# The Newton steps of the channel mixers' norm columns on VectorE in place of GpSimd

## The chip, the cores and the metric

The kernel runs on one core of a Trainium2 chip. The metric is the device time of one execution in microseconds, as the median of three runs. A core has a matrix engine (TensorE; PE in the profile, PEld its weight loads), VectorE (DVE), ScalarE (ACT), GpSimd (POOL) and SyncE (SP), which here issues the loads. Each engine works through its own instructions in order and waits for others by semaphores.

## The reference, cut to what matters

A decoder trunk of two layers on 512 tokens of width 1024, in float32. Each layer is a channel mixer, a token mixer and another channel mixer, so there are four channel mixers, numbered 0 to 3 (`idx` in the code):

```python
def rmsnorm(x, g):
    x32 = x.astype(jnp.float32)
    y = x32 * lax.rsqrt(jnp.mean(x32 * x32, axis=-1, keepdims=True) + RMS_EPS)
    return y.astype(x.dtype) * g

def swiglu(x, w_gate, w_up, w_down):
    return (jax.nn.silu(x @ w_gate) * (x @ w_up)) @ w_down

h = h + 0.5 * swiglu(rmsnorm(h, ffn_norm_a[i]), ...)   # before the token mixer
h = h + 0.5 * swiglu(rmsnorm(h, ffn_norm_b[i]), ...)   # after it
```

The hidden width of the channel mixers is 2816. The token mixers (latent attention in layer 0, sparse attention in layer 1) are not touched.

## The kernel before, in words

**Layout.** The residual stream `h` is held transposed: 8 tiles of 128 features by 512 tokens. A float32 product is made from three products of a high and a low part (`hi` is a rounded copy by ScalarE, `lo` the remainder, by a subtraction on VectorE). The weights are split in the same way: `wslab` (L132) loads a tile `wr`, ScalarE copies it (L143), VectorE makes the remainder (L145).

**The norm.** The products are made from the unnormed `h` (times the gains), and the factor 1/sqrt(mean square) of each token is applied afterwards. For a channel mixer the factor must be there as a `row`: 128 equal partitions by 512 tokens. It is made in these steps:

- squares and their sum over the features. In mixers 1 to 3 ScalarE squares, GpSimd adds into `s2` (L254), and `norm_col` (L273) sums over partitions on TensorE into 128x4 values `pc` (L278). In mixer 0, ScalarE squares the input in token order and sums along the row (L422), which gives the 128x4 values directly;
- `rsqrt` (L256): three instructions on VectorE (L259 to L261) make a first guess from the bits of the float, and three Newton steps refine it. Each round is four instructions on GpSimd (L264 to L267) where `pool` is set, three on VectorE (L269 to L271) where it isn't. All are on 128x4 values, in the tile `small`;
- `norm_bcast` (L286): eight TensorE instructions (four matmuls in the program, L290) spread the column over a PSUM bank `pb`, and ScalarE copies it to `row` (L450).

**Where this stands in a channel mixer** (`ffn`, L368). The first three of 22 hidden tiles are made by plain products (`plain`, L356: L364 to L366), gate and up for each, into `pg` and `pu`. In mixers 1 to 3 the column is asked for behind the two plain products of the first tile. In mixer 0 it is asked for behind those of the second. The broadcast stands on TensorE behind the second tile's products, and the third tile's follow it. The gate of each tile (L377 to L379) needs `row`. Meanwhile VectorE makes the operands of the remaining 19 tiles: `combine` (L236 to L238 and a split, L170 and L171) sums pieces of the activations, and `wsums` (L308, with L338 to L342) pieces of the weights, for a scheme of seven products in place of eight (L352 to L354). After that come the down projections (L162 to L164, added to `h` in L401).

**What sets the order.** The kernel is written through a framework that orders each engine's instructions by a planner: of the instructions that are ready, by its own model of time, the one that was written first goes first. So the order of VectorE's instructions is not the written one; where a short chain waits for its own last step, an instruction that is ready is put between. Buffers of a tag are used in turn: a weight tile's copy waits until TensorE has used the tile that it replaces.

Of the kernel before, what the change touches and what calls it, by code (L numbers as in the profile page):

```python
# [20 lines left out]
D = 1024  # L21
# [40 lines left out]
class Kern:  # L62
# [305 lines left out]
    def ffn(self, idx, gain_next, ap, tp):  # L368
# [5 lines left out]
        def gate(f, g):  # L374

            t = tg[f] = tp.tile([P, S], F32, tag="tg", bufs=2, name="tg")
            nc.vector.tensor_tensor(t, g, row, op=ALU.mult)  # L377
            nc.scalar.activation(t, t, AF.Silu, scale=-1.0)
            nc.vector.tensor_tensor(t, t, row, op=ALU.mult)  # L379
# [4 lines left out]
        def act(f):  # L384
            t = tu[f]
            if f < PLAIN:
                t = tu_tile()
                nc.vector.scalar_tensor_tensor(t, tu[f], -1.0, tg[f], op0=ALU.mult, op1=ALU.mult)
            else:
                nc.vector.tensor_tensor(t, t, tg[f], op=ALU.mult)  # L390
            ah[f] = ap.tile([P, S], F32R, tag="act", bufs=4 * NG, name="ah")
            al[f] = ap.tile([P, S], F32R, tag="act", bufs=4 * NG, name="al")
            self.split(t, ah[f], al[f])
# [19 lines left out]
        sums, xts = self.small_sums, []  # L413

        def tokens(t):

            xts.append(tp.tile([P, D], F32, tag="fr", bufs=3, name="xt"))
            with self.tc.issue_after(self.high.ins):
                nc.scalar.dma_start(xts[t], a["x_tok"][t * P : (t + 1) * P, :])

        def squares(t):
            nc.scalar.activation(xts[t], xts[t], AF.Square, accum_out=sums[:, t : t + 1])  # L422
# [7 lines left out]
        for f, g in enumerate(gates):  # L430
            u = tu[f] = self.bank(("mm", "S")[f % 2], "pu")
            self.plain(idx, f, 0, g)
            if f == 1 and idx == 0:

                squares(0)
                tokens(3)
                squares(1)
            self.plain(idx, f, 1, u)
            if f == 0:
                for c in self.late:  # L440
                    self.sumsq(self.h[c])
                col = self.norm_col(D, self.s2, pool=True) if idx else None
            elif f == 1:
                if idx == 0:
                    squares(2)
                    squares(3)
                    col = self.rsqrt_col(sums, D, pool=True)
                pb = self.norm_bcast(col)
                row = tp.tile([P, S], F32, tag="row", bufs=1, name="row")
                nc.scalar.activation(row, pb, AF.Copy)  # L450
                for e in range(2):
                    gate(e, gates[e])
                    act(e)
            else:
                gate(f, g)
                act(f)
            for p in (((0,), (1,), (2, 3)) if idx else ((0, 1), (2,), (3,)))[f]:
                self.combine(p)
# [842 lines left out]
```

## Time and profile before

| | us |
|---|---|
| median of three runs | 1926.41 |
| the runs | 1928.86, 1926.41, 1923.17 |
| span of the profiled execution | 1920.1 |
| TensorE busy | 1876.1 |
| VectorE busy | 1518.9 |
| ScalarE busy | 1091.4 |
| GpSimd busy | 334.9 |

The span runs from the first to the last instruction of one execution; the page has no device time of that execution beside it, and the three runs are 3.1 to 8.8 us above it. In a row of a timeline stand the start and the duration in us, the engine, the line of the kernel, the operation, the tile written and the tiles read, the shapes, and how often. A bracket is the time for which the engine was idle before, and what it waited for. A row of a list of waits has who waited for whom, the total in us, how often, and the longest.

### The profile page before, as it was taken

The page shows a single profiled execution, that of the slowest core. Times are in us where ns is not written, and L with a number is a line of the kernel's source. Part 1 is how long each engine was busy: PE and PEld are TensorE (multiplying, and loading weights), DVE is VectorE, ACT ScalarE, POOL GpSimd, SP SyncE. Part 2 cuts the span into 40 slices and gives each one's busy share as a digit, 9 for nine tenths or more (in the row PEclk, how much of TensorE's full clock was granted, in tenths as well). Part 3 has the DMA queues.
Part 4 walks back from the last instruction along what each step waited for, and adds up shares of the span by engine and source line. Part 5 has one row for each costly group of instructions (what it writes and reads, how often), then busy time and mean ns, then how long its engine had stood idle before and what let it go on. Part 6 is the DMA issues. An engine that isn't in the chain of part 4 may idle for free. (4 is left out here: it accounts for less than half of the span.)

```text
span 1920.1 us, 33220 instructions
## 1 busy us (share of the span) xinstructions
PE 1876.1 (98%) x12584; PEld 1707.3 (89%) x12584; DVE 1518.9 (79%) x2838; ACT 1091.4 (57%) x2040; POOL 334.9 (17%) x421
## 2 busy tenths in 40 slices
PE   8999999999999999999999999999999999999998
PEld 8999999878888999998999999877788888999997
DVE  7988886678778888876888888655987978888885
ACT  7555554478665555555555555435877865555553
POOL 1000000257631000002200000114666531000000
PEclk9999999999999999999999999999999999999999
DMA  6433321311233333323333332243122133333321
GB/s 224 140 100 99 113 90 42 110 50 42 73 116 111 100 100 109 112 62 107 117 110 108 104 100 79 65 123 100 51 67 67 40 118 96 108 112 108 104 76 67
DMA packets 75904, 183.28 MB, mean 95 GB/s; under 512 B 9040, under 2 KB 37072, under 8 KB 75744
## 3 DMA queue, kind: packets, MB, share of 16 engines
q1 hardware_dynamic: 72800, 176.39, 29.6%
q10 hardware_dynamic: 2944, 4.77, 0.7%
q8 instruction: 99, 1.62, 0.3%
q14 instruction: 61, 0.50, 0.1%
HBM read 178.96 MB, written 2.16 MB: 94 GB/s over the span
## 5 line engine op out<-in xcount | busy, mean ns | idle before, releaser
L254 POOL TENSOR_TENSOR s<-s,sq 128x512 f32<-128x512 f32 x38 | 55.7, 1466 | 988.2 <-ACT sq L250 985.2
L163 PE MATMUL pd<-al,wd 128*128 128x512 f32 x576 | 225.0, 391 | 0.0
L162 PE MATMUL pd<-ah,wd 128*128 128x512 f32 x576 | 224.8, 390 | 0.0
L164 PE MATMUL pd<-ah,wd 128*128 128x512 f32 x576 | 224.6, 390 | 0.0
L171 DVE TENSOR_TENSOR w<-wr,w 128x1024 fp32r<-128x1024 f32 x72 | 88.1, 1224 | 134.1 <-ACT w L170 134.1
L352 PE MATMUL px<-four,wh 128*128 128x256 f32 x608 | 168.5, 277 | 0.0
L354 PE MATMUL pq<-four,wl 128*128 128x256 f32 x608 | 167.9, 276 | 0.3 <-DVE wl L171 0.3
L354 PE MATMUL px<-four,wl 128*128 128x256 f32 x608 | 168.0, 276 | 0.0
L353 PE MATMUL px<-four,wh 128*128 128x256 f32 x608 | 167.9, 276 | 0.0
L352 PE MATMUL pq<-four,wh 128*128 128x256 f32 x608 | 167.9, 276 | 0.0
L353 PE MATMUL pq<-four,wh 128*128 128x256 f32 x608 | 167.8, 276 | 0.0
L143 ACT ACTIVATE w<-wr 128x1024 fp32r<-128x1024 f32 (+5 forms) x120 | 100.6, 844 | 104.7 <-issue 20.1
L401 DVE SCALAR_TENSOR_TENSOR h<-pd,h 128x512 f32<-128x512 f32 x216 | 148.0, 685 | 13.8 <-PE pd L164 13.7
L170 ACT ACTIVATE wd<-wdr 128x384 fp32r<-128x384 f32 x192 | 99.3, 519 | 101.4 <-ACT wd L170 62.9
L164 PEld LDWEIGHTS pd<-ah,wd 128*128 128x128 f32 x576 | 108.2, 188 | 22.9
L162 PEld LDWEIGHTS pd<-ah,wd 128*128 128x128 f32 x576 | 108.1, 188 | 20.3
L163 PEld LDWEIGHTS pd<-al,wd 128*128 128x128 f32 x576 | 108.1, 188 | 19.7
L145 DVE TENSOR_TENSOR w<-wr,w 128x1024 fp32r<-128x1024 f32 (+4 forms) x81 | 83.3, 1031 | 48.8 <-ACT w L143 48.2
L171 DVE TENSOR_TENSOR wd<-wdr,wd 128x384 fp32r<-128x384 f32 x192 | 105.7, 552 | 18.6 <-ACT wd L170 18.3
L639 ACT ACTIVATE p<-p,small 128x512 f32<-128x512 f32 (+1 forms) x192 | 106.8, 558 | 21.0 <-DVE small L638 17.3
L352 PEld LDWEIGHTS px<-four,wh 128*128 128x128 f32 x608 | 114.1, 188 | 0.9 <-ACT pg L477 0.5
L354 PEld LDWEIGHTS pq<-four,wl 128*128 128x128 f32 x608 | 114.1, 188 | 0.7 <-DVE wl L171 0.7
(359 smaller groups left out, 6281.1 us busy)
## 6 DMA issues: line engine op xcount, KB each, us to landing
wr<-in_w_gu SPq DMA_DIRECT2D x96, 512.0 KB, 3.3
ru<-in_w_gu SPq DMA_DIRECT2D x76, 512.0 KB, 4.2
wdr<-in_w_down SPq DMA_DIRECT2D x192, 192.0 KB, 2.4
wr<-in_w_down SPq DMA_DIRECT2D x24, 256.0 KB, 2.6
wr<-in_mla_w_o SPq DMA_DIRECT2D x8, 512.0 KB, 3.3
wr<-in_nsa_w_q SPq DMA_DIRECT2D x8, 512.0 KB, 3.3
th<-btab_d SPq DMA_DIRECT2D x16, 256.0 KB, 3.6
wr<-in_nsa_w_o SPq DMA_DIRECT2D x8, 512.0 KB, 3.6
```

The lines of the kernel that those rows point to most:

```text
L143: self.copied = nc.scalar.activation(wh[:, m], raw[:, m], AF.Copy)
L145: nc.vector.tensor_tensor(wl[:, m], raw[:, m], f32v(wh[:, m]), op=ALU.subtract)
L162: mm(out, wh, xh, start=first, stop=False)
L163: mm(out, wh, xl, start=False, stop=False)
L164: return mm(out, wl, xh, start=False, stop=last)
L170: nc.scalar.activation(hi, src, AF.Copy)
L171: (nc.gpsimd if pool else nc.vector).tensor_tensor(lo, src, f32v(hi), op=ALU.subtract)
L352: mm(out, wh[:, p], xh, start=first and p == 0, stop=False, skip_group_check=True)
L353: mm(out, wh[:, p], xl, start=False, stop=False, skip_group_check=True)
L354: mm(out, wl[:, p], xh, start=False, stop=last and p == KP - 1, skip_group_check=True)
L401: nc.vector.scalar_tensor_tensor(self.h[c], p, 0.5, self.h[c], op0=ALU.mult, op1=ALU.add)
L639: nc.scalar.activation(p_sb[:, :n], p_sb[:, :n], AF.Exp, bias=nm, scale=-1.0, accum_out=sm)
```

## The change

Both calls in `ffn` that set `pool=True` lose it: that of mixers 1 to 3 through `norm_col`, and that of mixer 0 directly. The twelve GpSimd instructions on 128x4 values per mixer (a square, a product, a scale and shift, a product, three times) become nine on VectorE, of the form that the token mixers' norms use already. No other call sets `pool` for the norm, so the GpSimd branch is not used any more.

```diff
             if f == 0:
                 for c in self.late:
                     self.sumsq(self.h[c])
-                col = self.norm_col(D, self.s2, pool=True) if idx else None
+                col = self.norm_col(D, self.s2) if idx else None
             elif f == 1:
                 if idx == 0:
                     squares(2)
                     squares(3)
-                    col = self.rsqrt_col(sums, D, pool=True)
+                    col = self.rsqrt_col(sums, D)
                 pb = self.norm_bcast(col)
```

The two forms of a round:

```python
            if pool:
                nc.gpsimd.tensor_tensor(t, y, y, op=ALU.mult)
                nc.gpsimd.tensor_tensor(t, t, v, op=ALU.mult)
                nc.gpsimd.tensor_scalar(t, t, -0.5, 1.5, op0=ALU.mult, op1=ALU.add)
                nc.gpsimd.tensor_tensor(y, y, t, op=ALU.mult)
                continue
            nc.vector.scalar_tensor_tensor(t, y, -0.5, v, op0=ALU.mult, op1=ALU.mult)
            nc.vector.tensor_tensor(t, t, y, op=ALU.mult)
            nc.vector.scalar_tensor_tensor(y, t, 1.5, y, op0=ALU.add, op1=ALU.mult)
```

## The prediction

> **What bounds the kernel now.** I read the page's busy shares first, to see which engine has no room.
>
> ```profile
> span 1920.1 us, 33220 instructions
> PE 1876.1 (98%) x12584; PEld 1707.3 (89%) x12584; DVE 1518.9 (79%) x2838; ACT 1091.4 (57%) x2040; POOL 334.9 (17%) x421
> ```
>
> TensorE is busy for 1876.1 of 1920.1 us, so only 44 us of gaps can be won by moving work. VectorE has 401 us of idle time over the whole span, but that is an average. The next view is the list of waits of TensorE, and of its weight loads (PEld): total us, how often, the longest.
>
> ```profile
> PE pb L290 <- POOL small L267: 10.6, 4, 4.2
> PE pg L364 <- ACT w L143: 5.8, 1, 5.8
> ...
> PEld pb L290 <- POOL small L267: 11.4, 4, 4.4
> ```
>
> The largest wait of TensorE is on exactly the instructions that the change touches: four times it stands before the broadcast of the norm column (L290) until the last Newton step on GpSimd (L267) is done, 10.6 us in all (11.4 counted at the weight loads). The timeline of TensorE gives the four places. Each bracket is the idle time in front.
>
> ```profile
> 31.64 1.16 PE L290 MATMUL pb<-ident,small 128*128 128x128 f32 x8 [1.11 <-POOL small L267]
> 591.04 1.16 PE L290 MATMUL pb<-ident,small 128*128 128x128 f32 x8 [2.51 <-POOL small L267]
> 932.72 1.16 PE L290 MATMUL pb<-ident,small 128*128 128x128 f32 x8 [2.79 <-POOL small L267]
> 1591.08 2.07 PE L290 MATMUL pb<-ident,small 128*128 128x128 f32 x8 [4.18 <-POOL small L267]
> ```
>
> So TensorE was free at 30.53, 588.53, 929.93 and 1586.90 us. I call these places 1 to 4, one for each channel mixer. Why the column is late shows in the timeline of GpSimd, here the first and the last of the twelve steps at places 1 and 4:
>
> ```profile
> 25.11 0.20 POOL L264 TENSOR_TENSOR small<-small 128x4 f32<-128x4 f32 x1 [24.67 <-DVE small L261]
> ...
> 31.39 0.20 POOL L267 TENSOR_TENSOR small<-small 128x4 f32<-128x4 f32 x1
> ...
> 1580.30 6.39 POOL L264 TENSOR_TENSOR small<-small 128x4 f32<-128x4 f32 x1 [9.82 <-DVE small L261]
> ...
> 1590.83 0.20 POOL L267 TENSOR_TENSOR small<-small 128x4 f32<-128x4 f32 x1
> ```
>
> A step on 4 columns takes 0.20 us when it is free, but at place 4 the first one took 6.39. It ended at 1586.69. The timeline of VectorE for the same time shows what ended it:
>
> ```profile
> 1578.45 0.15 DVE L259 TENSOR_SCALAR small<-pc 128x4 f32<-128x4 f32 x1
> 1578.52 0.41 DVE L237 TENSOR_TENSOR u<-y,u 128x256 f32<-128x256 f32 x1
> 1578.85 0.16 DVE L260 TENSOR_SCALAR small<-small 128x4 int32<-128x4 int32 x1
> 1578.92 1.22 DVE L171 TENSOR_TENSOR wl<-ru,wh 128x1024 fp32r<-128x1024 f32 x1
> 1580.06 0.16 DVE L261 TENSOR_SCALAR small<-small 128x4 int32<-128x4 int32 x1
> 1580.13 1.22 DVE L145 TENSOR_TENSOR w<-wr,w 128x1024 fp32r<-128x1024 f32 x1
> 1581.26 1.22 DVE L171 TENSOR_TENSOR four<-u,four 128x1024 fp32r<-128x1024 f32 x1
> 1582.40 0.42 DVE L238 TENSOR_TENSOR u<-y,u 128x256 f32<-128x256 f32 x1
> 1582.73 0.68 DVE L171 TENSOR_TENSOR wl<-s,wh 128x512 fp32r<-128x512 f32 x1
> 1583.34 1.02 DVE L171 TENSOR_TENSOR wd<-wdr,wd 128x384 fp32r<-128x384 f32 x2
> 1584.28 1.22 DVE L171 TENSOR_TENSOR four<-u,four 128x1024 fp32r<-128x1024 f32 x1
> 1585.41 1.21 DVE L145 TENSOR_TENSOR w<-wr,w 128x1024 fp32r<-128x1024 f32 x1
> 1587.96 0.56 DVE L171 TENSOR_TENSOR wd<-wdr,wd 128x384 fp32r<-128x384 f32 x1 [1.34 <-ACT wd L170]
> ```
>
> From 1580.13 to 1586.62 VectorE runs two-input subtractions without a gap, and the first GpSimd step ends within 0.1 us of the first pause. GpSimd's steps are held up while VectorE is dense. [...]
>
> **The change part by part.** Removed: 4 x 12 steps on GpSimd, and with them TensorE's wait on L267. Added: 4 x 9 steps on VectorE (L269 to L271, three a round). No DMA moves, and nothing is moved past SP's queue. The price of the added steps is in the trace, since the token mixers already run this chain on VectorE:
>
> ```profile
> 359.37 0.16 DVE L269 SCALAR_TENSOR_TENSOR small<-small 128x4 f32<-128x4 f32 x1
> ...
> 359.84 1.23 DVE L145 TENSOR_TENSOR w<-wr,w 128x1024 fp32r<-128x1024 f32 x1
> 360.99 0.16 DVE L269 SCALAR_TENSOR_TENSOR small<-small 128x4 f32<-128x4 f32 x1
> ...
> 361.97 0.16 DVE L271 SCALAR_TENSOR_TENSOR small<-small 128x4 f32<-128x4 f32 x1
> ```
>
> The last six steps start between 360.99 and 361.97: 0.98 / 5 = 0.196 us from step to step. Nine in a row are 1.77 us. Where another instruction that is ready stands between two steps, a step holds VectorE for less: L259 to L237 above is 0.07 us, L260 to L171 0.07. So nine steps cost VectorE between 9 x 0.07 = 0.63 us (interleaved) and 1.77 us (in a row), per place.
>
> *Is the column in time?* In a row, the steps at place 4 would end at about 1580.06 + 0.20 + 1.77 = 1582.0, 4.9 us before TensorE is free. At worst the planner puts one ready instruction between any two steps, as it does with L259, L260 and L261 here. Eight ready instructions lie behind L261 (two in the row marked x2), which end at 1586.62. With eight steps between them at 0.07 that is 1587.2, and with a ninth behind them 1587.4: 0.5 us after 1586.90. I carry this worst case to all four places: a wait of 0 to 2.0 us stays of the 10.6. I take 0.3, near the low end, since at the other places fewer instructions stand before VectorE's pause, or TensorE comes later. Gain here: 10.3 us, between 8.6 and 11.4.
>
> *What stands behind the steps on VectorE?* The remainders of the weights (L145), which TensorE needs. At place 2 TensorE already waits for one:
>
> ```profile
> 581.65 0.16 DVE L261 TENSOR_SCALAR small<-small 128x4 int32<-128x4 int32 x1
> 581.72 1.21 DVE L145 TENSOR_TENSOR w<-wr,w 128x1024 fp32r<-128x1024 f32 x1
> ...
> 582.99 0.39 PE L366 MATMUL pu<-x,w 128*128 128x256 f32 x1 [0.78 <-DVE w L145]
> ```
>
> If all nine steps went ahead of this L145, TensorE would lose 1.77 us more there. At place 4 the same L145 ends at 1581.35, about when the product that uses it begins (1586.90 minus the 5.5 us from 582.99 to 588.53, a whole product less its first instructions). So two places are exposed, 3.5 us together. But L145 stands directly behind L261, that is, it was ready then, and takes the slot in which the first step waits for L261. I take 0.5 us of loss, between 0 and 3.5. The other instructions of the list are put off by 0.6 us or so, and the next product's L145 (1585.41) still ends before TensorE needs it behind the broadcast.
>
> [...]
>
> *The clock.* The granted clock is the third column from the right (here of TensorE alone; busy us, instructions, clock, DMA share, GB/s):
>
> ```profile
> 934.00:937.40 3.40, 3.40 (x18) 0.51 0.29 111
> 938.00:941.40 3.40, 3.40 (x33) 1.00 0.00 0
> 1592.90:1596.10 3.20, 3.20 (x17) 0.50 0.03 8
> 1597.00:1600.20 3.20, 3.20 (x31) 1.00 0.00 0
> ```
>
> Right after the gaps of 2.79 and 4.18 us TensorE ran at half clock for 3.4 us and more. It did 18 matmuls where 33 fit: (1 - 18/33) x 3.40 = 1.55 us lost. At place 4: (1 - 17/31) x 3.20 = 1.45, and the broadcast took 2.07 for 1.16: 0.91. Together 3.9 us that go with the gaps. Between 0 (if these halvings have another cause) and 3.9. I take 3.9, because both start at the gap.
>
> *Sum:* 10.3 - 0.5 + 3.9 = 13.7 us, 1920.1 to 1906.4 of span. What lies around the span isn't on the page. The three runs (1923.17, 1926.41, 1928.86) are 3.1, 6.3 and 8.8 above it; I take the median's 6.3: 1906.4 + 6.3 = **1912.7 us**. By the bounds alone the gain is between 8.6 - 3.5 = 5.1 and 11.4 + 3.9 = 15.3: 1911.1 to 1921.3.
>
> **The rivals.**
>
> *The clock stays.* The stalls go but the half-clock stretches turn up elsewhere. For it: the gap of 2.51 us at place 2 brought none. Against: both stretches follow a gap at once. 10.3 - 0.5 = 9.8 gained: 1916.6. [...]
>
> *Given back later.* TensorE comes earlier and then waits for VectorE, which makes the operands of the next products. For it is the stretch after place 1:
>
> ```profile
> 31.60:60.00 28.40, 28.07 (x214) 26.26 (x215) 26.91 (x40) 18.48 (x30) 0.00 (x0) 1.00 0.33 103
> ```
>
> VectorE is busy 26.91 of 28.40 us there. Against: that is only place 1, worth 1.11 us, and the page's 79% leaves room at the others. If all were given back: 1926.4, no change; if only place 1's, 1913.8, inside the forecast.
>
> *A worse queue (slower).* VectorE works in order. If the last step lands behind the L145 of the product after the broadcast, the column waits for TensorE itself, since that weight's copy on ScalarE waits until the product before has freed its tile:
>
> ```profile
> 588.62 1.06 ACT L143 ACTIVATE w<-wr 128x1024 fp32r<-128x1024 f32 x1 [2.15 <-PE pu L366]
> 589.71 1.22 DVE L145 TENSOR_TENSOR w<-wr,w 128x1024 fp32r<-128x1024 f32 x1 [1.80 <-ACT w L143]
> ```
>
> From TensorE's end (588.53) to the end of that L145 (590.93) are 2.4 us, and each step behind it adds 0.2. With five steps behind, 3.4 us at each place, 13.6 for 10.6: 3.0 lost, and half clock at all four (about 2 us each, 8 for 3.9): 4.1 more. That is 1933.5. It decides from one step behind that L145 at every place; with one, it is 10.4 for 10.6, no change. Against: the steps come from earlier lines than that product, and VectorE pauses for 1.80 us before it.
>
> *The change does nothing*, since the flag is ignored: excluded, because the branch in rsqrt picks the engine by it. But the planner of the order may place other instructions anew, worth a few us either way; that stands in the ends of the range.
>
> **How the numbers follow.** Forecast 0.60 (1912.7, own range 1909 to 1919). The clock stays 0.15 (1916.6). Given back or the wait kept 0.18 (1926). Worse queue 0.07 (1933.5). A difference of 0.3% is 5.8 us, about what a measurement can tell here: under 1920.6 is faster. Faster: 0.60 + 0.15 + some 0.04 of the third case that gives only part back = 0.79. Same: 0.14. Slower: 0.07. The range goes down to the low bound 1911.1 less 3 us of scatter, as between the runs shown, 1908; and up past the bound of 1921.3 by the same, 1924. Outside it lie the slower case and most of the full giving back, 0.2.
>
> **What would show it.** Right: no wait of TensorE on L267, and on L271 under 1 us over the four places; L269 to L271 x36 more (12 to 48) at about 0.16 us; GpSimd without the twelve-step groups; full clock around places 3 and 4; the product in front of the broadcast not later than before. Wrong: a wait of TensorE on L271 of 2.4 us or more with an L145 in front of the last step (worse queue); new waits on L145, L171 or pg of the size of the gain (given back); or half-clock stretches without a gap before them.

## The result, and the profile after

The changed kernel takes 1910.45 us (median of four runs, 1908.63 to 1912.97). The kernel before takes 1925.87 in the runs beside them (1923.17 to 1928.86). The ratio is 0.9925, with a 95% interval of 0.9907 to 0.9944: 10.8 to 17.9 us less. The forecast was 1912.7 us.

The page after begins:

```profile
span 1909.3 us, 33207 instructions
PE 1873.7 (98%) x12584; PEld 1704.4 (89%) x12584; DVE 1522.4 (80%) x2874; ACT 1091.0 (57%) x2040; POOL 301.7 (16%) x373
```

VectorE has 36 instructions more and 3.5 us more work. GpSimd has 48 fewer. TensorE does the same 12584 matmuls in 2.4 us less, and its idle time falls from 44.0 to 35.6 us.

In TensorE's list of waits the line with L267 is gone. What is left there (total, times, longest) stands under VectorE's last step, and the token mixers have 0.9 us of it:

```profile
PE pb L290 <- DVE small L271: 2.2, 3, 1.3
```

The timeline of TensorE at the four places, and at some points between them:

```profile
30.17 1.05 PE L290 MATMUL pb<-ident,small 128*128 128x128 f32 x8
...
587.03 1.13 PE L290 MATMUL pb<-ident,small 128*128 128x128 f32 x8
...
925.79 1.05 PE L290 MATMUL pb<-ident,small 128*128 128x128 f32 x8
...
946.60 0.39 PE L352 MATMUL pg<-x,wh 128*128 128x256 f32 x1 [0.23 <-ACT pg L484]
...
1255.70 0.80 PE L164 MATMUL pcm<-x,w 128*128 128x512 f32 x1 [1.95 <-DVE w L145]
...
1275.49 0.46 PE L988 MATMUL pkc<-hid,w 128*128 128x128 f32 x2 [0.29 <-issue]
...
1569.03 0.95 PE L278 MATMUL pc<-ones,s 128*128 128x1 f32 x8
...
1582.45 1.13 PE L290 MATMUL pb<-ident,small 128*128 128x128 f32 x8 [1.32 <-DVE small L271]
```

Three places have no wait any more. Place 4 keeps 1.32 us. The same points of the kernel before that the prediction doesn't show:

```profile
954.75 0.38 PE L352 MATMUL pg<-x,wh 128*128 128x256 f32 x1 [0.20 <-ACT pg L484]
...
1263.69 0.50 PE L164 MATMUL pcm<-x,w 128*128 128x512 f32 x1 [1.72 <-DVE w L145]
...
1282.27 0.46 PE L988 MATMUL pkc<-hid,w 128*128 128x128 f32 x2 [0.24 <-issue]
...
1574.83 0.95 PE L278 MATMUL pc<-ones,s 128*128 128x1 f32 x8
```

The difference of two starts is the lead of the changed kernel. It says where the time went:

| point | lead, us | won since the point before |
|---|---|---|
| broadcast, place 1 | 1.47 | 1.47 |
| broadcast, place 2 | 4.01 | 2.54 |
| broadcast, place 3 | 6.93 | 2.92 |
| 20 us behind place 3 | 8.15 | 1.22 (half clock) |
| start of the sparse mixer (L164) | 7.99 | -0.16 |
| 20 us later (L988) | 6.78 | -1.21 |
| column sums, mixer 3 (L278) | 5.80 | -0.98 |
| broadcast, place 4 | 8.63 | 2.83 |
| end of the span | 10.8 | 2.2 (half clock) |

The clock behind places 3 and 4 is full now (busy us and instructions of PE, PEld, DVE, ACT and POOL; clock; DMA share; GB/s). But the first row is the start of the sparse mixer, where the changed kernel has half clock from 1255.55 us on (0.69 is the mean of the row) and the kernel before (second fence) had none:

```profile
1254.00:1258.00 4.00, 2.29 (x5) 1.82 (x6) 3.45 (x11) 0.00 (x0) 0.00 (x0) 0.69 1.06 306
925.79:950.00 24.21, 23.83 (x199) 23.10 (x198) 22.60 (x32) 15.40 (x25) 0.00 (x0) 1.00 0.32 106
1582.45:1600.00 17.55, 17.55 (x151) 17.30 (x152) 15.44 (x22) 10.78 (x19) 0.00 (x0) 1.00 0.28 97
```

```profile
1262.00:1266.00 4.00, 2.31 (x10) 1.93 (x11) 3.46 (x11) 0.00 (x0) 0.00 (x0) 1.00 1.05 313
```

On VectorE the nine steps at place 4 stand between the other instructions:

```profile
1574.29 0.16 DVE L261 TENSOR_SCALAR small<-small 128x4 int32<-128x4 int32 x1
1574.36 1.22 DVE L145 TENSOR_TENSOR w<-wr,w 128x1024 fp32r<-128x1024 f32 x1
1575.49 0.16 DVE L269 SCALAR_TENSOR_TENSOR small<-small 128x4 f32<-128x4 f32 x1
1575.57 1.22 DVE L171 TENSOR_TENSOR four<-u,four 128x1024 fp32r<-128x1024 f32 x1
...
1581.29 0.16 DVE L270 TENSOR_TENSOR small<-small 128x4 f32<-128x4 f32 x1
1581.67 0.56 DVE L171 TENSOR_TENSOR wd<-wdr,wd 128x384 fp32r<-128x384 f32 x1 [0.23 <-ACT wd L170]
1582.15 0.16 DVE L271 SCALAR_TENSOR_TENSOR small<-small 128x4 f32<-128x4 f32 x1
```

A step holds VectorE for 0.07 to 0.08 us, but the chain lasts 8.0 us from L261 to the end of L271, since after each step an instruction that is ready comes first. The last step lies behind an L171 that waited 0.23 us for ScalarE.

### The profile page after: what moved, and what is told of

Read it like the earlier page. It is cut to its first block, busy times and chain, and to the rows that moved or that the text cites. A ratio compares the mean times of both kernels' runs of the same rounds, so it can differ in the third digit from the quotient of the medians.

```text
span 1909.3 us, 33207 instructions
## 1 busy us (share of the span) xinstructions
PE 1873.7 (98%) x12584; PEld 1704.4 (89%) x12584; DVE 1522.4 (80%) x2874; ACT 1091.0 (57%) x2040; POOL 301.7 (16%) x373
## 4 chain that ended last, share of the span: by engine, by line
PE 81%; DVE 8%; ACT 5%; issue 3%; POOL 2%; DMA 1%; SPq 0%; ACTq 0%; POOLq 0%; DVEq 0%
PE pd L164 8%; PE pd L163 8%; PE pd L162 8%; PE px L352 5%; PE px L353 5%; PE px L354 5%; PE pg L352 4%; PE pg L353 4%; PE pg L354 4%; PE pq L354 4%; PE pq L353 4%; PE pq L352 4%; PE o L604 2%; PE pt L593 1%; ACT p L639 1%
## 5 line engine op out<-in xcount | busy, mean ns | idle before, releaser
L164 PE MATMUL pd<-ah,wd 128*128 128x512 f32 x576 | 224.7, 390 | 0.0
L171 DVE TENSOR_TENSOR w<-wr,w 128x1024 fp32r<-128x1024 f32 x72 | 88.2, 1224 | 131.9 <-ACT w L170 131.9
L164 PEld LDWEIGHTS pd<-ah,wd 128*128 128x128 f32 x576 | 108.2, 188 | 22.9
L145 DVE TENSOR_TENSOR w<-wr,w 128x1024 fp32r<-128x1024 f32 (+4 forms) x81 | 83.3, 1031 | 47.4 <-ACT w L143 46.8
L171 DVE TENSOR_TENSOR wd<-wdr,wd 128x384 fp32r<-128x384 f32 x192 | 105.5, 550 | 19.4 <-ACT wd L170 19.3
```

The costliest lines, as they stand in the source:

```text
L145: nc.vector.tensor_tensor(wl[:, m], raw[:, m], f32v(wh[:, m]), op=ALU.subtract)
L164: return mm(out, wl, xh, start=False, stop=last)
L171: (nc.gpsimd if pool else nc.vector).tensor_tensor(lo, src, f32v(hi), op=ALU.subtract)
```

## The experiments

**Is it the wait, or the engine?** The steps stay on GpSimd, and the broadcast with what hangs on it is asked for one product later.

```diff
             self.plain(idx, f, 0, g)
+            if f == 2:
+                pb = self.norm_bcast(col)   # row, gates and acts of tiles 0 and 1 with it
             self.plain(idx, f, 1, u)
...
             elif f == 1:
-                pb = self.norm_bcast(col)
```

> The Newton steps stay on GpSimd, but the broadcast of the column, the copy to row and the gates of the first two tiles are asked for one plain product later (5.5 us of matmuls between the column's start and its use are added). Theory (the wait): the change won only because TensorE no longer stands idle for the column, so covering the column with work should win as much. TensorE's wait on L267 falls from 10.6 us to under 0.5, the clock is full around places 3 and 4, the first GpSimd step at place 4 still takes about 6.4 us, and the time is within 3 us of the changed kernel (1908 to 1914). Rival (the engine): GpSimd's steps cost more than their wait, by holding up VectorE beside them, or the later row delays the gates and their PSUM banks; then at least 4 us of the gain stay away (over 1914), with new waits of TensorE on pg or on VectorE.

Measured: 1907.39 us, ratio to the kernel before 0.9911 (0.9896 to 0.9926). GpSimd is as slow as ever at place 4 (first and last step):

```profile
1570.82 6.39 POOL L264 TENSOR_TENSOR small<-small 128x4 f32<-128x4 f32 x1 [9.82 <-DVE small L261]
...
1581.41 0.20 POOL L267 TENSOR_TENSOR small<-small 128x4 f32<-128x4 f32 x1
```

But TensorE doesn't notice, with no wait at any of the four places; here the fourth:

```profile
1582.71 1.05 PE L290 MATMUL pb<-ident,small 128*128 128x128 f32 x8
```

The theory holds: the whole gain comes with the column covered, on either engine. The time is even 0.6 us below the range given.

The same with the steps on VectorE:

> The changed kernel with the same later broadcast. Theory: the 1.3 us that TensorE still waits at place 4 go as well, so about 1.3 us less than the changed kernel (1909), with no wait on L271 at the four places. Rival: row comes 5.5 us later and the gates with it, TensorE waits for a bank or an operand afterwards, and the time is 2 us or more above the changed kernel.

Measured: 1908.83 us, 0.9921 (0.9907 to 0.9934), no wait at the four places. The later row costs TensorE up to 0.7 us behind place 1, on a copy of ScalarE into pg, and no more.

**How much of the chain is covered?** Fewer steps, and more.

```diff
-        for _ in range(3):
+        for _ in range(self.rounds):   # 2 or 6 in the channel mixers, 3 elsewhere
```

> The changed kernel with two Newton rounds in place of three in the channel mixers (the third refinement is left out, which is part of the computation). Theory: VectorE's added steps are hidden except at place 4, so only the 1.3 us there go: 1909 and no wait on L271. Rival (VectorE is the bound around the places): each step left out counts, 12 steps of 0.16 us = 1.9 us, and the waits on L145 and L171 at the places get shorter.

Measured: 1907.69 us, 0.9913 (0.9896 to 0.993), and no wait at the four places; place 4:

```profile
1579.69 1.05 PE L290 MATMUL pb<-ident,small 128*128 128x128 f32 x8
```

As the theory has it. The time alone can't tell the two expectations apart, and both let the wait on L271 go. The waits on L145 tell them apart: the rival has them shorter, and TensorE's longest one at place 2 is 0.75 us here and 0.77 in the changed kernel.

> The changed kernel with six Newton rounds (nine more steps at each place, the same value). Theory: the steps go between VectorE's other instructions, so the column ends later by nine slots, 0.2 to 1.2 us each, past the end of the product that covered it. At places 2 to 4 TensorE waits on L271 for 1.5 to 4 us each, more where a step lands behind the second L145; half clock returns after the longest wait; 6 to 12 us above the changed kernel (1916 to 1923). Rival: nine more short steps are covered like the first nine, and the time stays within 3 us of the changed kernel.

Measured: 1915.49 us, 0.9953 (0.9938 to 0.9968), some 5 us above the changed kernel, a little under the range.

```profile
36.22 1.16 PE L290 MATMUL pb<-ident,small 128*128 128x128 f32 x8
...
589.23 1.13 PE L290 MATMUL pb<-ident,small 128*128 128x128 f32 x8 [1.77 <-DVE small L271]
929.58 1.13 PE L290 MATMUL pb<-ident,small 128*128 128x128 f32 x8 [1.48 <-DVE small L271]
...
1585.40 1.92 PE L290 MATMUL pb<-ident,small 128*128 128x128 f32 x8 [2.46 <-DVE small L271]
```

The waits are 1.77, 1.48 and 2.46 us, at the low end of the range or just under it. With them half clock comes back behind place 4 (third number from the end):

```profile
1586.00:1588.00 2.00, 2.00 (x12) 2.00 (x11) 0.41 (x2) 0.63 (x2) 0.00 (x0) 0.50 0.34 84
```

At place 1 the planner put the broadcast one product later by itself (36.22), so nothing waits there. At places 2 to 4 no step fell behind the L145 of the product after the broadcast, which follows directly on the last step (589.00, 929.35 and 1585.17). The rival is out: the cover ends somewhere between nine and eighteen steps, and at place 4 before nine.

**What makes GpSimd late?** VectorE is thinned out around place 4: remainders are written as copies by ScalarE (the subtraction is left out; the line numbers are three higher).

```diff
-            (nc.gpsimd if pool else nc.vector).tensor_tensor(lo, src, f32v(hi), op=ALU.subtract)
+            if self.thin:   # mixer 3, up to its fourth hidden tile
+                nc.scalar.activation(lo, src, AF.Copy)
+            else:
+                (nc.gpsimd if pool else nc.vector).tensor_tensor(lo, src, f32v(hi), op=ALU.subtract)
```

> The kernel before, with GpSimd's steps, but around place 4 (mixer 3, up to its fourth hidden tile) the remainders of the activations' sums, of the weights' sums and of the down weights are written as a copy by ScalarE in place of the subtraction on VectorE (that part of the computation is left out; the whole time isn't read). Theory (VectorE's dense two-input work holds GpSimd up): with VectorE sparse the first GpSimd step at place 4 ends at VectorE's first pause, within 3 us of its start in place of 6.4, the twelve steps are over in under 7 us, and TensorE waits for the column under 1.5 us there. Rival (GpSimd is slow by itself after a long idle time, 9.8 us at that place): the first step takes about 6.4 us as before.

The first and the last of GpSimd's steps, and VectorE where it pauses:

```profile
1579.92 1.11 POOL L267 TENSOR_TENSOR small<-small 128x4 f32<-128x4 f32 x1 [8.20 <-DVE small L264]
...
1584.60 0.20 POOL L270 TENSOR_TENSOR small<-small 128x4 f32<-128x4 f32 x1
```

```profile
1582.06 0.42 DVE L241 TENSOR_TENSOR u<-y,u 128x256 f32<-128x256 f32 x1
1586.01 1.23 DVE L145 TENSOR_TENSOR w<-wr,w 128x1024 fp32r<-128x1024 f32 x1 [3.52 <-ACT w L143]
```

The first step takes 1.11 us after 8.2 us of idle time, the twelve steps 4.9 us in place of 10.7, and TensorE has no wait at place 4. From 1582.62 on, beside a resting VectorE, each step takes 0.20. Slowness after idle time is out: the first step had 8.20 us of it here and 9.82 in the kernel before. What holds GpSimd up is VectorE's work beside it. It ends even before VectorE's first long pause, in the cracks between sparser instructions, so "until the first pause" was too strict.

**GpSimd without cover, beside a sparse VectorE.** The four norms of the token mixers get `pool=True` as well, in the kernel before.

> The kernel before, with the Newton steps of the token mixers' four norms on GpSimd too. VectorE is sparse there. Theory: twelve steps at 0.28 us from start to start, 3.4 us, and up to 1.2 us more for each VectorE instruction that falls beside them, against 1.8 to 2.8 us on VectorE; no first step of 3 us or more where VectorE rests. TensorE waits for the column 1 to 4 us more in all. Rival (slow after idle): first steps of 3 us and more at these places as well.

One run gave 1936.52 us beside 1924.05 for the kernel before. A chain in the latent mixer (first and last step), and TensorE at the four norms:

```profile
362.60 1.11 POOL L264 TENSOR_TENSOR small<-small 128x4 f32<-128x4 f32 x1 [7.56 <-DVE small L261]
...
366.59 0.20 POOL L267 TENSOR_TENSOR small<-small 128x4 f32<-128x4 f32 x1
```

```profile
366.84 1.16 PE L290 MATMUL pb<-ident,small 128*128 128x128 f32 x8 [2.92 <-POOL small L267]
...
385.96 2.08 PE L290 MATMUL pb<-ident,small 128*128 128x128 f32 x8 [2.76 <-POOL small L267]
...
411.42 1.16 PE L290 MATMUL pb<-ident,small 128*128 128x128 f32 x8 [2.23 <-POOL small L267]
...
1279.73 2.08 PE L290 MATMUL pb<-ident,small 128*128 128x128 f32 x8 [2.86 <-POOL small L267]
```

The durations are as the theory has them: 3.3 to 4.2 us for the chains, no first step over 1.2. The size of the wait was missed: 10.8 us over the four norms, where the kernel before has 1.0 in its list of waits, so 9.8 more, and 1 to 4 were expected. So where nothing covers the chain the engine does matter, by about 2.4 us for each.

**The parts.** Mixer 3 alone, and mixers 0 to 2 alone.

```diff
-                col = self.norm_col(D, self.s2, pool=True) if idx else None
+                col = self.norm_col(D, self.s2, pool=idx < 3) if idx else None    # m3only
+                col = self.norm_col(D, self.s2, pool=idx == 3) if idx else None   # m012, with mixer 0 on VectorE
```

> Only mixer 3 (place 4) has its steps on VectorE. Theory: 4.18 - 1.32 of wait and 2.4 of half clock: 5.2 us less than the kernel before, with the waits at places 1 to 3 as before (1.1, 2.5, 2.8). Rival (half clock isn't tied to the gap): 2.9 us less.

> Mixers 0 to 2 (places 1 to 3) have their steps on VectorE, mixer 3 on GpSimd. Theory: 1.11 + 2.51 + 2.79 of wait and 1.55 of half clock: 8.0 us less than the kernel before, with about 4.2 us of wait and half clock at place 4. With the kernel that changes mixer 3 alone this adds up to the whole change. Rival: the parts do not add up, by more than 4 us, since the gain of one place is given back at a later one.

Measured: mixer 3 alone 1916.6 us, 0.995 (0.993 to 0.9969); mixers 0 to 2 alone 1916.29, 0.9945 (0.9924 to 0.9967). The kernel before had 1925.22 (1921.61 to 1930.35) beside them. By medians that is 8.6 and 8.9 us, together 17.5 for the 15.4 of both, within what the intervals leave open. For mixer 3 both figures, 5.2 and 2.9 us, were too low: the interval is 6 to 13 us. What the rest of its gain is stays open. What was to be decided by them, whether half clock is tied to the gap, its profile shows: with 1.15 us left at place 4 the clock is full behind it, and the four profiles with 4.18 to 4.30 us there all have half clock. Place 4 of the first kernel and of the second, which keeps its wait:

```profile
1590.62 1.13 PE L290 MATMUL pb<-ident,small 128*128 128x128 f32 x8 [1.15 <-DVE small L271]
...
1585.80 2.08 PE L290 MATMUL pb<-ident,small 128*128 128x128 f32 x8 [4.24 <-POOL small L267]
```

And place 1 of the first, which is the same code as before, has 2.51 us where the profile of before had 1.11:

```profile
33.45 1.16 PE L290 MATMUL pb<-ident,small 128*128 128x128 f32 x8 [2.51 <-POOL small L267]
```

**The kernel before, once more.**

> The kernel before, profiled again with the device time of the same execution, for the term that was put around the span. Theory: the execution's time is 1.9 us above its span, as for the changed kernel, and the kernel's executions differ by stretches of half clock; the four gaps are the same within 0.3 us. Rival: the time is about 6 us above the span, as the prediction took it.

This execution took 1923.82 us with a span of 1922.0, so 1.8 us lie around the span, not 6.3; over the 31 executions of this kernel with both numbers on record it is 1.7 to 1.8. For the changed kernel it is 1911.18 with 1909.3, 1.9. The gaps are 1.14, 2.51, 2.79 and 4.26. But this time the gap at place 2, of the same 2.51 us, brought half clock, and in the first profile it didn't (second fence):

```profile
589.00:593.10 4.10, 2.45 (x11) 2.45 (x12) 1.23 (x1) 0.61 (x2) 1.42 (x3) 0.66 0.58 211
```

```profile
588.00:592.00 4.00, 1.49 (x14) 1.29 (x12) 1.22 (x1) 1.06 (x1) 2.44 (x7) 1.00 0.45 134
```

**Changed kernel and later broadcast side by side.**

> The changed kernel on the same chip as the two kernels with the later broadcast. Theory: place 4 keeps a wait of 1.3 us on L271, no other place has one over 0.3 us, and the time is 1 to 3 us above both; with that the later broadcast is worth at most what place 4 still waits, and the engine of the steps is worth nothing beside it. Rival: one of the two kernels with the later broadcast is 4 us or more away, so that the engine or the later row matters by itself.

> The steps on GpSimd with the later broadcast, once more. Theory: 1 to 3 us below the changed kernel, no wait on L267. Rival: equal to it or above, and the earlier difference was that of the chip.

> The steps on VectorE with the later broadcast, once more. Theory: 1 to 3 us below the changed kernel, and within 2 us of the same kernel with the steps on GpSimd. Rival: further apart than that.

Measured on one chip, beside 1924.14 us for the kernel before: the change 1909.99 (ratio 0.9927, 0.991 to 0.9945), the later broadcast with GpSimd 1907.45 (0.9914, 0.9897 to 0.9931), with VectorE 1909.17 (0.9923, 0.9903 to 0.9944). The changed kernel waits 1.16 us at place 4, the two others nowhere at the four places. The later broadcast with the steps on GpSimd, that is, without the change, has the lowest median both times, 2.5 us under the changed kernel here. The two intervals overlap, but both carry the scatter of the kernel before. Run against run, the later broadcast with GpSimd is lower in 33 of the 36 pairs, so it is likely the faster one, by a few us at most. With VectorE it is only 0.8 under, and lower in 23 of 36 pairs, which shows nothing.

## Why the prediction was right, and where it wasn't

- *What bounds the kernel* (TensorE, standing idle for the column): right, and shown from both sides. Cover the wait and the same gain comes without the change (the later broadcast with GpSimd); lengthen the chain and the wait returns (six rounds).
- *The price of the steps*: 0.07 to 0.08 us of VectorE when interleaved, as taken: L269 at 1575.49 lasts 0.16 us, and L171 starts 0.08 us after its start. The count is 36 more, as said, but from 36 to 72 (12 to 24 for each line); the prediction's 12 to 48 was wrong.
- *Is the column in time?* At place 4 the planner did what was called the worst case, one instruction between any two steps; at place 2 some steps stand in a row. Places 1 to 3 were in time, as the 0.3 us taken near the low end had it. At place 4 the wait is 1.32 us, over the 1 us that the prediction named for all four places as a sign of being right, and its bound for that place was 0.5: the chain took 8.0 us from L261 where 7.3 had been counted, since the last step fell behind one L171 more, the one in front of which VectorE rests, waiting for ScalarE. Over all four places the wait kept is within the 2.0 us, but the 0.3 us taken were a quarter of it.
- *What stands behind the steps*: no loss showed. L145 kept its slot directly behind L261, and the waits on L145 at place 2 are 0.78 us before and 0.77 after (not shown here).
- *The clock*: right at places 3 and 4, where 1.22 and some 2.2 us came back (3.4 of 3.9). In part that was luck: the same gap of 2.79 us at place 3 brought half clock in four of five profiles that have it. What failed is the thought that the clock only gives: 1.2 us went again at the start of the sparse mixer, where a gap of 1.95 us that stood there before too (1.72) now met half clock. That is no single case: half clock stands behind that gap in seven of the nine profiles of kernels whose steps or broadcast were moved at places 1 to 3, and in none of the five others. Why is open, since the gap is much the same in both (1.32 to 1.95 and 1.47 to 1.72 us). So of the rival "the clock stays" one stretch came true, and the others went with their gaps. Another 1.0 us was lost over that mixer's attention; 0.55 us of it goes at one wait (L1085, 1.24 us for 0.56), and the cause is open.
- *What lies around the span*: wrong. 6.3 us were taken, and 1.8 to 1.9 were measured. The profiled execution of before was at the low end: 1920.1 + 1.9 = 1922.0, 3.9 under the median of its runs. So the span came out at 1909.3, not 1906.4 (2.9 less won), and this term 4.4 us lower. The two errors had opposite signs, so that the sum came within 2.3 us of the median is partly luck. Seen from the runs: 15.4 = 10.8 between the spans + 3.9 for the low execution of before + 0.7 for that after.
- *Why the kernel before varies more* (1919.29 to 1930.35 over all runs shown, the changed one 1908.63 to 1912.97): its time goes with the granted clock. Of the 31 executions on record, the four with a mean clock of 0.996 took 1920.3 us on average, the seven with 0.993 1927.3, the one with 0.990 1930.35. The profiles of it or of kernels equal to it at that place show where this can come from: a gap at place 1 of 1.11 to 3.11 us, and half clock behind place 2 in three of five. That these places make up the whole spread was not shown.
- *Given back later* and *a worse queue*: neither came at three rounds, but for the half clock in the sparse mixer. At six rounds the column is late as in the second, by 1.5 to 2.5 us, though no step stands behind the L145 named there.

## What to carry to other kernels

Read who waits, and what covers the wait, before choosing an engine. Here the engine of twelve tiny steps was worth 15 us only because their result was asked for too early, and asking for it 5.5 us later gave at least as much. Where nothing can cover a short chain, VectorE's steps (0.2 us apart) beat GpSimd's (0.28, and one third more of them), by about 2.4 us at each of the four norms here. Beside a dense VectorE, GpSimd was a poor place for the chain: 10.7 us at place 4, and 4.9 with VectorE thinned out. Before adding a span's difference to a median, look up where in the spread of its runs the profiled execution lies.

## What the runs showed of the hardware

- Twelve GpSimd instructions on 128x4 values, of 0.20 us each when alone, took 10.7 us at place 4, where VectorE ran two-input subtractions without a gap for the first 6.3 us. The first step alone took 6.39 us and ended 0.07 us after the last of these; it took 1.11 when VectorE was thinned out.
- Half clock isn't a matter of the gap's length alone: a gap of 2.51 us brought it in one execution and not in another. In each profile the half-clock stretches begin on one grid of 3.41 us, and all but the one at the very end of the span last one or two of its steps. In the first profile of the kernel before they begin at 934.10, 1326.63 and 1589.46 us, which is 115 and 77 steps apart. The gaps sort by how much of them falls into one step. Of the 25 gaps of over 1.2 us in front of a broadcast, in all profiles, the 17 with 1.94 us or more in one step brought half clock, and the 8 with 1.69 us or less did not. The gap of 2.51 us at place 2 of the kernel before has 2.15 us in one step in the second profile, where half clock followed, and 1.69 in the first, where none did. It doesn't hold everywhere: at the start of the sparse mixer a gap of 1.32 us in all was enough in the profile with six rounds, and 1.72 us in one step was not in the first profile of the kernel before.
- With the token mixers' norms on GpSimd, gaps of 2.23 to 2.92 us in front of their four broadcasts brought half clock: single matmuls of 128x512 behind each took 0.63 us, where they took 0.39 to 0.40 at full clock.
